# Weight sums released block by block, output stores on ScalarE's queue, and two buffers for the second group's blocks

## The chip, the cores and the metric

The kernel runs on one core of a Trainium2 chip. A core has TensorE (PE, matrix products), VectorE (DVE), ScalarE (ACT), GpSimd (POOL) and SyncE (SP), which here issues every transfer between the chip's main memory (DRAM) and the on-chip memory (SBUF). Products accumulate in PSUM banks. Each engine works through its own list of instructions in order; semaphores tie the lists together. The metric is the time of one execution in device microseconds, the median of several runs.

## The reference

One layer of an encoder works on two sequences, a prompt of 1024 tokens and a sample of 256, with a model width of 2048, all in float32:

```python
hn = rmsnorm(x, norm_w)
proj = jnp.einsum('btd,dp->btp', hn, w_in)          # 9232 columns
att = neighbourhood_attention(na_q, na_k, na_v, na_rpb)   # 8 heads of 128
att = (att * jax.nn.silu(na_g)).astype(x.dtype)
qk = jax.nn.silu(centred_depthwise_conv(ml_qk, conv_w, conv_b))
h = bidirectional_mlstm(mq, mk, mv, gates)          # 4 heads of 256
h = rmsnorm(h, head_norm_w)
mem = (h * jax.nn.sigmoid(ml_o) * jax.nn.silu(ml_z)).astype(x.dtype)
mixed = jnp.concatenate([att, mem], axis=-1)
y = x + jnp.einsum('btm,md->btd', mixed, w_out)     # then a final rmsnorm
```

The attention lets a token on a grid 64 wide see a window of 8 rows and 16 columns, with a learned bias. The mLSTM is a gated linear recurrence, done forwards and backwards in chunks.

## The kernel before

Each float32 operand is split into a high and a low half (`split`, lines 151 to 157: ScalarE copies the high half on line 153, VectorE takes the difference on line 154), and a product is three matmuls of halves. The 1280 tokens are worked on in a first part of 768 and a second of 512. Large products use a seven-product scheme for 2x2 blocks (Strassen-Winograd), which needs sums and differences of blocks of both operands.

The stages, in the order of the program:

1. The first part's projections (`first_tiles`, `pair_a`), until about 1120 us. Results go to DRAM tensors `pT`, `vD`, `cD`.
2. A loop over `ML_H` = 4 (line 1160). Turn i projects the second part's columns for two attention heads and one mLSTM head (`proj_v`, `proj_pair`, matmuls on lines 497 and 579; weights through two buffers tagged `wraw`), and then `run` (line 1134) weaves two streams together: the mLSTM units of head i and the attention of heads 2i and 2i+1. An attention head is one sample unit, `setup`, and four prompt blocks (`block`, line 707). A block scores, takes the softmax, transposes, multiplies by the values into a PSUM bank `b`, and writes its gated result (lines 750 and 753); the fourth stores the head to `mixT` (line 755).
3. After each `run`, eight calls of `wsum_unit` (line 1146). A unit loads 512 KB of the output weights `w_os` into the only buffer of tag `wsum`, forms four sums and differences on GpSimd in place (lines 1151 to 1154), and stores them to `sD` (line 1156). All 32 units prepare the block sums of the output weights.
4. `late_gate`: gate projections of the second part, multiplied into `mixT` (lines 548 and on). Between them `build` prepares the sums of the activations for the first output group of 512 tokens, through one buffer `bld` (line 1192), into tiles of the pool `comb`, which takes the place of the attention pool `att`.
5. The output projection (line 1265): group 0 for both column pairs (`G00`, `G01`), then the 256 sample tokens (`S`, whose activations `xs` are loaded on line 1374 through the buffers `po`), then group 1 (`G10`, `G11`), whose blocks are built in pieces during and after `S`. `w_tiles` loads and splits weights; `put` adds the products to `y` and the residual `xr`; `done` squares on ScalarE into a `po` buffer `jk`; `finish` (line 1293) scales a row of tiles by the norm and stores it on line 1305.

The order of the instructions on each engine is not written by hand. A scheduler fixes it at build time by simulating the program: an instruction is placed when its inputs and its buffer are free in the simulation and its engine is idle. Everything inside `run` has raised priority; the weight sums have not, and depend on nothing but their buffer. Tiles with one tag share that tag's buffers, and a new tile waits until all work on the old one in its buffer is over. On the chip each engine follows the fixed order, whatever comes late.

The lines that the change touches are the units and the place that calls them, the blocks of attention, the two masks (lines 462 to 465), `build`, `finish`, and the number of `po` buffers, `NPO`, on line 29.

Of the kernel before, what the change touches and what calls it, by code (L numbers as in the profile page):

```python
# [8 lines left out]
F32 = mybir.dt.float32  # L9
F32R = mybir.dt.float32r  # L10
AF = mybir.ActivationFunctionType
ALU = mybir.AluOpType

P = 128
# [11 lines left out]
HALF = GA // 2  # L26
NU = 8
VW = 258
NRA, NWS, NWT, NPC, NPO = 3, 8, 4, 5, 5
NAK = 384  # L30
KC0 = (0, 8, 24, 32)
BKIND = (0, 1, 1, 2)
# [6 lines left out]
def kernel(  # L39
# [24 lines left out]
    def f(ap):  # L64
        return ap.bitcast(F32)
# [390 lines left out]
    for _ in bg:  # L456
# [2 lines left out]
    wb, xp0 = pools  # L459

    late = ctx.enter_context(tc.tile_pool(name="late", bufs=1))
    mask_f, mask_b = (
        tri(late.tile([P, P], F32, tag=n, name=n), cm, 0, (0.0, NEG))
        for n, cm in (("mask_f", -1), ("mask_b", 1))
    )

    xp1 = ctx.enter_context(tc.tile_pool(name="xp1", bufs=1))

# [129 lines left out]
    att_ctx = ExitStack()  # L598
    ap = att_ctx.enter_context(tc.tile_pool(name="att", bufs=2))

    def hf(name):
        return ap.tile([P, 1032], F32R, tag="hf", name=name, bufs=8)

# [25 lines left out]
    def na_transpose(nm, st, order, dst):  # L629
        b = bank("a", f"{nm}t")  # L630
        n = len(order)
        for i, c in enumerate(order):
            PE.transpose(b[:, i * P : (i + 1) * P], st[:, c * P : (c + 1) * P], ident)
        bv = b[:, : n * P].rearrange("p (k q) -> p k q", q=P)
        S.copy(dst[0], bv)
        V.tensor_tensor(dst[1], bv, f(dst[0]), op=ALU.subtract)

    def na_sample(h):
        nm = f"nas{h}"
# [43 lines left out]
    def na_prompt(h):  # L683
        nm = f"nap{h}"
        hd = {}

        def setup():
            t = na_tile("nqk", [P, 4, TP], f"{nm}qk", 1, F32R)
            q, k = ([t[:, 2 * i + z] for z in range(2)] for i in range(2))
            for half in range(2):  # L690
                cs = slice(half * 512, half * 512 + 512)
                for w_, t, src in (("q", q, pT[QT0 + h]), ("k", k, pT[KT0 + h])):
                    raw = na_tile("nraw", [P, 512], f"{nm}{w_}r{half}", 2)
                    DM.dma_start(raw, src[:, cs])
                    if w_ == "q":
                        d = [
                            x_[:, cs].rearrange("p (b r c) -> p r b c", b=4, c=16) for x_ in t
                        ]
                        split(*d, raw.rearrange("p (r b c) -> p r b c", b=4, c=16))
                    else:  # L700
                        split(t[0][:, cs], t[1][:, cs], raw)
            o = na_tile("not", [P, TP], f"{nm}o", 1)
            DM.dma_start(o[:, :GA], pT[GT0 + h][:, :GA])
            hd["q"], hd["k"], hd["o"] = q, k, o
            yield

        def block(c4):
            q, k = hd["q"], hd["k"]
            n2 = f"{nm}_{c4}"
            kc = KC0[c4]  # L710
            kv = [x_.rearrange("p (r c) -> p r c", c=64) for x_ in k]
            st = [
                na_softmax(
                    f"{n2}_{rh}",
                    lambda a_: q[a_][:, rh * 512 + c4 * P : rh * 512 + (c4 + 1) * P],
                    lambda b_: kv[b_][:, 4 * rh : 4 * rh + 12, kc : kc + 32],
                    NAK, h, (BKIND[c4] * 2 + rh) * NAK,
                )
                for rh in range(2)
            ]  # L720
            v = na_tile("nv", [P, 2, 512], f"{n2}v", 2, F32R)
            raw = na_tile("nraw", [P, 512], f"{n2}vr", 2)
            vs = vD[h // 2][:TP, (h % 2) * P : (h % 2 + 1) * P].rearrange("(r c) d -> r c d", c=64)
            for m in range(4):
                DM.dma_start(raw[:, m * P : (m + 1) * P], vs[4 * m : 4 * m + 4, kc : kc + 32, :])
            split(v[:, 0], v[:, 1], raw)
            yield
            pt = na_tile("npt", [P, 2, 768], f"{n2}pt", 1, F32R)
            for rh in range(2):
                na_transpose(  # L730
                    f"{n2}_{rh}", st[rh], ((1, 2, 0), (0, 1, 2))[rh],
                    [
                        pt[:, z].rearrange("p (s r q) -> p s r q", r=2, q=P)[:, :, rh, :]
                        for z in range(2)
                    ],
                )
            yield
            b = bank("a", f"{n2}o")
            parts = ((1, 0, 256, 0), (2, 256, 256, 0), (0, 512, P, 0), (3, 640, P, P))
            for j, (m, src, n, o) in enumerate(parts):  # L740
                for i, (a_, b_) in enumerate(((0, 0), (0, 1), (1, 0))):
                    PE.matmul(
                        b[:, o : o + n], v[:, a_, m * P : (m + 1) * P], pt[:, b_, src : src + n],
                        start=j == 0 and i == 0, stop=j == 3 and i == 2,
                    )
            ov = hd["o"].rearrange("p (r c) -> p r c", c=64)
            bv = b[:, :256].rearrange("p (r c) -> p r c", c=16)
            cs = slice(c4 * 16, c4 * 16 + 16)
            ng = GA // 64
            V.scalar_tensor_tensor(  # L750
                ov[:, :ng, cs], bv[:, :ng], 0.5, ov[:, :ng, cs], op0=ALU.mult, op1=ALU.mult
            )
            S.copy(ov[:, ng:, cs], bv[:, ng:])
            if c4 == 3:
                DM.dma_start(mixT[h][:, :TP], hd["o"])
            yield

        yield setup()
        for c4 in range(4):
            yield block(c4)  # L760
# [382 lines left out]
                        if next(u_, "end") == "end":  # L1143
                            act.remove(u_)

    def wsum_unit(u):
        cp, kk, half = u // 16, u // 2 % 8, u % 2
        t = ap.tile([P, 4, 256], F32, tag="wsum", name=f"wsum{u}", bufs=1)
        DM.dma_start(t.rearrange("p s c -> p (s c)"), w_os[u])
        a11, a12, a21, a22 = (t[:, i] for i in range(4))  # L1150
        G.tensor_tensor(a22, a21, a22, op=ALU.add)  # L1151
        G.tensor_tensor(a21, a11, a21, op=ALU.subtract)
        G.tensor_tensor(a11, a22, a11, op=ALU.subtract)
        G.tensor_tensor(a12, a12, a11, op=ALU.subtract)  # L1154
        c0 = kk * 512 + half * 256
        DM.dma_start(sD[cp][:, :, c0 : c0 + 256], t)

    X = LazyX()
    rbs[1] = late.tile([P, GB], F32, tag="rstdb1", name="rstdb1")
    for i in range(ML_H):  # L1160
        proj_v(4 + i, X)
        if i == 0:
            x_stats(1, lambda c: mid(f"xdg1_{c}", 256))
        for n in (QK0 + 8 + 2 * i, QK0 + 2 * i):
            proj_pair(n, X)
        if i == 0:
            with tc.high_priority():
                tris = ml_tris()
                gates = {sq: ml_gates(sq, tris) for sq in ("p", "s")}
        proj_v(i, X)  # L1170
        for n in (QT0 + 2 * i, KT0 + 2 * i):
            proj_pair(n, X)
        run(
            [u for sq in ("s", "p") for u in ml_units(sq, i, gates[sq])],
            [u for h in (2 * i, 2 * i + 1) for u in (na_sample(h), *na_prompt(h))],
        )
        for u in range(8 * i, 8 * i + 8):
            wsum_unit(u)
    att_ctx.close()
    comb = ctx.enter_context(tc.tile_pool(name="comb", bufs=1))  # L1180
    SG = 256
# [7 lines left out]

    def build(g, C, kk, parts):  # L1190
        nm = f"bd{g}{parts[0]}{kk}"
        bl = comb.tile([P, 1024], F32, tag="bld", name=nm)
        s0, s1 = bl[:, :512], bl[:, 512:]
        for z, s_ in enumerate((s0, s1)):
            DM.dma_start(s_, mixT[kk + 8 * z][:, g * 512 : g * 512 + 512])
        for kind in parts:
            C[kind, kk] = comb_tile(kind, kk, f"cm{g}")
        b11, b12, d1, t3 = s0[:, :SG], s0[:, SG:], s1[:, :SG], s1[:, SG:]

        def put(kind, src):  # L1200
            t = C[kind, kk]
            if kind != "b":
                t = t.rearrange("p h c t -> p h (c t)")
            split(t[:, 0], t[:, 1], src)

        if "b" in parts:
            put("b", b11)
        if "u" in parts:
            put("u", s1)
        if "w" in parts:  # L1210
            V.tensor_tensor(s1, s1, s0, op=ALU.subtract)
        else:
            V.tensor_tensor(t3, t3, b12, op=ALU.subtract)
        if "v" in parts:
            V.tensor_tensor(b12, b12, b11, op=ALU.subtract)
            V.tensor_tensor(b11, t3, b11, op=ALU.add)
            put("v", s0)
        if "w" in parts:
            V.tensor_tensor(d1, d1, t3, op=ALU.subtract)
            put("w", s1)  # L1220
# [72 lines left out]
    def finish(t):  # L1293
# [5 lines left out]
        for i in range(D // w_):  # L1299
# [2 lines left out]
                S.mul(yt[:, cs], yt[:, cs], rs)  # L1302
            else:
                V.tensor_scalar(yt[:, cs], yt[:, cs], rs, None, op0=ALU.mult)
            DM.dma_start(y[t * P : (t + 1) * P, cs], yt[:, cs])

    def add(o, a_, b_):
        V.tensor_tensor(o, a_, b_, op=ALU.add)
# [179 lines left out]
```

## Time and profile before

| what | value |
|---|---|
| median of 3 runs | 2721.89 us (2718.3 to 2723.4) |
| the profiled execution | 2715.22 us, span 2713.5 us |
| instructions | 43634 |
| mean granted TensorE clock | 0.987 |
| TensorE busy | 96% of the span |
| VectorE, ScalarE, GpSimd busy | 72%, 51%, 27% |
| moved by DMA | 454.21 MB, mean 167 GB/s |

The span is cut into rows of instructions, each with a start and a length. A line of the views below names the engine, the source line, the operation and the tiles it writes and reads. Where an engine sat idle, the view of waits names the instruction that ended the idle time; "idle before" is that time. `SPq` is the queue on which SP issues transfers; a transfer's own landing appears as `DMA`. The granted clock is a share of TensorE's full speed.

### The profile page before, as it was taken

What the parts mean: (1) busy time and instruction counts of PE and PEld (TensorE: products, weight loads), DVE (VectorE), ACT (ScalarE), POOL (GpSimd) and SP (SyncE); (2) the same over time, 40 slices, a digit from 0 to 9 for tenths busy, and PEclk for the clock granted to TensorE, in tenths of its full rate; (3) what the DMA queues carried; (4) which work ended last, traced back from release to release, by engine and by line L of the source; (5) the groups of instructions that cost most, each with busy time, mean ns of one, the idle gap of its engine ahead of it and who ended that gap; (6) DMA issues with size and microseconds to landing.
All of it is one profiled execution on the core that took longest, in us unless ns stands there. A gap on an engine that the chain in (4) does not pass through costs nothing.

```text
span 2713.5 us, 43634 instructions
## 1 busy us (share of the span) xinstructions
PE 2611.9 (96%) x14518; PEld 2386.9 (88%) x14518; DVE 1963.3 (72%) x3902; ACT 1385.1 (51%) x3132; POOL 731.5 (27%) x1025
## 2 busy tenths in 40 slices
PE   8999999999999999988989999999999999989997
PEld 8999999999999999977878989889888887867776
DVE  7867878788787878863677587677676675777786
ACT  7534444444444444522645565665565443555554
POOL 0434444444444444233233210000010000120112
PEclk9999999999999999999989999999999999999999
DMA  6423333322323232656767755655655456778875
GB/s 208 149 74 123 110 126 106 98 94 94 106 94 106 90 105 93 205 187 205 246 209 232 246 176 178 204 168 170 197 159 160 148 187 230 217 232 264 285 234 181
DMA packets 258042, 454.21 MB, mean 167 GB/s; under 512 B 30320, under 2 KB 138008, under 8 KB 257816
## 3 DMA queue, kind: packets, MB, share of 16 engines
q1 hardware_dynamic: 257816, 451.42, 51.5%
q8 instruction: 114, 1.87, 0.3%
q14 instruction: 112, 0.92, 0.1%
HBM read 368.41 MB, written 82.91 MB: 166 GB/s over the span
## 4 chain that ended last, share of the span: by engine, by line
PE 35%; DMA 14%; DVE 5%; ACT 3%; POOL 2%; issue 2%; SPq 1%; POOLq 0%; ACTq 0%; DVEq 0%
PE pc L497 14%; PE G01p L1265 3%; PE G11p L1265 3%; PE G00p L1265 3%; PE pv L579 2%; DMA wsum<-in_w_os_dram 2%; DMA sD<-wsum 2%; PE G10p L1265 1%; PE S L1265 1%; DMA wr<-in_w_in_dram 1%; PE A52b L190 1%; DMA pT<-pco 1%; DMA nap_0vr<-vD 1%; POOL wsum L1154 1%; DMA bd1b<-mx 1%
## 5 line engine op out<-in xcount | busy, mean ns | idle before, releaser
L154 DVE TENSOR_TENSOR ws<-wr,ws 128x512 fp32r<-128x512 f32 x224 | 161.1, 722 | 96.0 <-ACT ws L153 94.5
L153 ACT CAST ws<-wr 128x512 fp32r<-128x512 f32 x224 | 138.0, 619 | 139.4 <-PE pc L497 81.6
L1288 POOL TENSOR_TENSOR y<-y,fn 128x512 f32<-128x512 f32 x40 | 61.7, 1554 | 522.0 <-ACT jk L1287 491.0
L1151 POOL TENSOR_TENSOR wsum<-wsum 128x256 f32<-128x256 f32 x32 | 26.5, 828 | 240.7 <-DMA wsum<-in_w_os_dram 204.3
L154 DVE TENSOR_TENSOR wsv<-wr_v,wsv 128x512 fp32r<-128x512 f32 x64 | 46.1, 726 | 30.8 <-ACT wsv L153 30.5
L1265 PE MATMUL S<-ws_S,xsb 128*128 128x512 f32 x192 | 48.9, 410 | 13.1 <-ACT xsb L153 10.7
L154 DVE TENSOR_TENSOR ws_G01w<-wrG01w,ws_G01w 128x512 fp32r<-128x512 f32 x56 | 44.5, 807 | 20.0 <-ACT ws_G01w L153 18.6
L1265 PEld LDWEIGHTS S<-ws_S,xsb 128*128 128x128 f32 x192 | 37.0, 196 | 24.5 <-ACT xsb L153 11.1
L153 ACT CAST wsv<-wr_v 128x512 fp32r<-128x512 f32 x64 | 38.8, 614 | 38.2 <-DMA wr_v<-in_w_in_dram 24.0
L154 DVE TENSOR_TENSOR ws_G11w<-wrG11w,ws_G11w 128x512 fp32r<-128x512 f32 x56 | 44.9, 820 | 16.5 <-ACT ws_G11w L153 16.1
L153 ACT CAST ws_G11w<-wrG11w 128x512 fp32r<-128x512 f32 x56 | 34.6, 619 | 36.6 <-PE G11p L1265 29.8
L153 ACT CAST ws_G01w<-wrG01w 128x512 fp32r<-128x512 f32 x56 | 34.7, 620 | 35.3 <-PE G01p L1265 28.5
L154 DVE TENSOR_TENSOR ws_S<-wrS,ws_S 128x512 fp32r<-128x512 f32 x64 | 46.2, 739 | 7.6 <-ACT ws_S L153 7.2
L276 DVE SCALAR_TENSOR_TENSOR pcv<-pco,cw_sb,pcv 128x516 f32<-128x516 f32 x64 | 49.0, 774 | 3.4 <-ACT pcv L270 3.3
L154 DVE TENSOR_TENSOR ws_G00w<-wrG00w,ws_G00w 128x512 fp32r<-128x512 f32 x48 | 37.1, 789 | 15.1 <-ACT ws_G00w L153 13.7
L1265 PE MATMUL S<-ws_S,xsv 128*128 128x512 f32 x192 | 46.2, 396 | 1.2 <-ACT ws_S L153 1.0
L497 PE MATMUL pc<-x_10h,ws 128*128 128x512 f32 x112 | 45.6, 407 | 0.0
L1265 PEld LDWEIGHTS S<-ws_S,xsv 128*128 128x128 f32 x192 | 35.7, 188 | 11.1 <-ACT ws_S L153 1.9
L154 DVE TENSOR_TENSOR ws_G10w<-wrG10w,ws_G10w 128x512 fp32r<-128x512 f32 x56 | 40.0, 742 | 7.1 <-ACT ws_G10w L153 7.0
L497 PE MATMUL pc<-x_11h,ws 128*128 128x512 f32 x112 | 45.2, 403 | 0.0
L153 ACT CAST ws_G00w<-wrG00w 128x512 fp32r<-128x512 f32 x48 | 29.6, 620 | 30.2 <-PE G00p L1265 27.6
L497 PE MATMUL pc<-x_0h,ws 128*128 128x512 f32 x112 | 45.0, 401 | 0.0
(1737 smaller groups left out, 9168.9 us busy)
## 6 DMA issues: line engine op xcount, KB each, us to landing
wr<-in_w_in_dram SPq DMA_DIRECT2D x112, 512.0 KB
wr_v<-in_w_in_dram SPq DMA_DIRECT2D x32, 512.0 KB
wsum<-in_w_os_dram SPq DMA_DIRECT2D x32, 512.0 KB
sD<-wsum SPq DMA_DIRECT2D x32, 512.0 KB
wrS<-in_w_o_dram SPq DMA_DIRECT2D x64, 256.0 KB
xq<-in_xtok_dram SPq DMA_DIRECT2D x20, 512.0 KB
xr<-in_xtok_dram SPq DMA_DIRECT2D x40, 256.0 KB
wrG00w<-sD SPq DMA_DIRECT2D x32, 256.0 KB
```

The lines of the kernel that those rows point to most:

```text
L153: S.copy(hi, src)
L154: V.tensor_tensor(lo, src, f(hi), op=ALU.subtract)
L190: PE.matmul(o, w(a_), x(b_), start=first and m == 0, stop=last and m == 2)
L276: V.scalar_tensor_tensor(dst[:, a:n], src[:, a + j - pad : n + j - pad], cw_sb[:, ct, j : j + 1], dst[:, a:n], op0=ALU.mult, op1=ALU.add,)
L497: PE.matmul(pb[j], t[:, wi, c : c + P], xs, start=r == 0 and f_ == 0 and q == 0 and wi == 0 and xs is xh, stop=r == 3 and f_ == 1 and q == ...
L579: PE.matmul(outs[tt], xs[:, tt * P : (tt + 1) * P], t[:, wi, q * w : (q + 1) * w], start=first and m == 0 and (gates or tt % 2 == 0), stop ...
L1151: G.tensor_tensor(a22, a21, a22, op=ALU.add)
L1154: G.tensor_tensor(a12, a12, a11, op=ALU.subtract)
L1265: PE.matmul(bk[s_], x_[:, xi, s_ * P : (s_ + 1) * P], t[:, wi, :512], start=first and m == 0, stop=last and m == 2,)
L1288: G.tensor_tensor(yc, yc, fn[nb], op=ALU.mult)
```

## The change

- `wsum_unit` moves ahead of the attention code and takes a second argument, `pace`. Before its load it copies one column of `pace` into its buffer on ScalarE. Each attention block calls one unit, number 4h + c4 for block c4 of head h, with its own PSUM bank as `pace`, right after its last copy. The eight calls after each `run` are gone. The sums run inside `run`, at its priority.
- `finish` first scales all pieces of a row and then stores them, last piece first, and the stores are issued by ScalarE.
- `build` for the second group takes one of the two `wraw` buffers for odd blocks and `bld` for even ones.
- `NPO` goes from 5 to 6. The masks `mask_f` and `mask_b` move from the pool `late` to the pool `att`.

```diff
-NRA, NWS, NWT, NPC, NPO = 3, 8, 4, 5, 5
+NRA, NWS, NWT, NPC, NPO = 3, 8, 4, 5, 6
...
     late = ctx.enter_context(tc.tile_pool(name="late", bufs=1))
-    mask_f, mask_b = (
-        tri(late.tile([P, P], F32, tag=n, name=n), cm, 0, (0.0, NEG))
-        for n, cm in (("mask_f", -1), ("mask_b", 1))
-    )
...
     ap = att_ctx.enter_context(tc.tile_pool(name="att", bufs=2))
 
+    mask_f, mask_b = (
+        tri(ap.tile([P, P], F32, tag=n, name=n, bufs=1), cm, 0, (0.0, NEG))
+        for n, cm in (("mask_f", -1), ("mask_b", 1))
+    )
...
+    def wsum_unit(u, pace):
+        cp, kk, half = u // 16, u // 2 % 8, u % 2
+        t = ap.tile([P, 4, 256], F32, tag="wsum", name=f"wsum{u}", bufs=1)
+        S.copy(t[:, 0, 0:1], pace)
+        DM.dma_start(t.rearrange("p s c -> p (s c)"), w_os[u])
+        a11, a12, a21, a22 = (t[:, i] for i in range(4))
+        G.tensor_tensor(a22, a21, a22, op=ALU.add)
+        G.tensor_tensor(a21, a11, a21, op=ALU.subtract)
+        G.tensor_tensor(a11, a22, a11, op=ALU.subtract)
+        G.tensor_tensor(a12, a12, a11, op=ALU.subtract)
+        c0 = kk * 512 + half * 256
+        DM.dma_start(sD[cp][:, :, c0 : c0 + 256], t)
...
             S.copy(ov[:, ng:, cs], bv[:, ng:])
+            wsum_unit(4 * h + c4, b[:, 0:1])
             if c4 == 3:
                 DM.dma_start(mixT[h][:, :TP], hd["o"])
...
-        for u in range(8 * i, 8 * i + 8):
-            wsum_unit(u)
     att_ctx.close()
...
-        bl = comb.tile([P, 1024], F32, tag="bld", name=nm)
+        if g and kk % 2:
+            bl = wb.tile([P, 1024], F32, tag="wraw", name=nm, bufs=2)
+        else:
+            bl = comb.tile([P, 1024], F32, tag="bld", name=nm)
...
                 V.tensor_scalar(yt[:, cs], yt[:, cs], rs, None, op0=ALU.mult)
-            DM.dma_start(y[t * P : (t + 1) * P, cs], yt[:, cs])
+        for i in reversed(range(D // w_)):
+            cs = slice(i * w_, i * w_ + w_)
+            S.dma_start(y[t * P : (t + 1) * P, cs], yt[:, cs])
```

The old `wsum_unit(u)`, without the copy and the argument, is removed from its place behind `run`.

11 lines of the change are left out of this document (removed).

## The prediction

> **What bounds the kernel now.** I read the page first, then the busy time by stretch, then who waits for whom on TensorE and on SP's queue, then the timelines round the longest waits. The page says who is nearest to full:
>
> ```profile
> span 2713.5 us, 43634 instructions
> PE 2611.9 (96%) x14518; PEld 2386.9 (88%) x14518; DVE 1963.3 (72%) x3902; ACT 1385.1 (51%) x3132; POOL 731.5 (27%) x1025
> ```
>
> TensorE is idle for 2713.5 - 2611.9 = 101.6 us, and only that can be won without removing matmuls; the change removes none. The same table by stretch (columns: stretch; busy us of PE, weight load, DVE, ACT, POOL; granted clock; share of the DMA engines; GB/s) shows where it lies:
>
> ```profile
> 1120.00:1300.00 180.00, 160.29 (x912) 140.03 (x911) 97.92 (x230) 61.84 (x121) 57.62 (x97) 0.94 0.62 204
> 1300.00:1600.00 300.00, 278.94 (x1748) 252.25 (x1747) 207.71 (x484) 176.71 (x436) 86.54 (x164) 0.96 0.70 226
> 1600.00:2140.00 540.00, 533.06 (x3251) 474.05 (x3250) 379.29 (x977) 331.27 (x811) 44.06 (x143) 1.00 0.55 172
> 2420.00:2540.00 120.00, 105.67 (x436) 82.20 (x436) 87.15 (x148) 67.01 (x131) 18.68 (x18) 0.96 0.80 265
> 2540.00:2714.00 174.00, 154.77 (x657) 121.92 (x655) 127.26 (x196) 88.98 (x164) 33.18 (x30) 0.97 0.70 233
> ```
>
> Idle is 19.7 us in 1120 to 1300 and 21.1 in 1300 to 1600, but 6.9 in the 540 us after that (0.013 per us), although the same attention and projection work runs there. Then 14.3 and 19.2 us in the output stage. The 32 weight sums run exactly in the two poor stretches. Their row, and the chain of waits, which in that stretch is a string of load, sum, store (first and thirteenth load of the string):
>
> ```profile
> L1149 SPq DMA_DIRECT2D wsum<-in_w_os_dram x32: 327/333/438, 1126.2 to 1558.6; - x32
> 1126.17 4.83 DMA wsum<-in_w_os_dram
> 1270.65 3.63 DMA wsum<-in_w_os_dram
> ```
>
> Twelve units between these two make (1270.65 - 1126.17) / 12 = 12.0 us a unit: with one buffer the units follow each other, each issued by SP in order. TensorE's waits there, and SP's own waits at the units' two DMAs:
>
> ```profile
> PE nas_0s L616 <- ACT nas0qk L153: 8.1, 1, 8.1
> PE mgsa L839 <- DVE mgstmp L833: 4.8, 1, 4.8
> PE mls_0s L920 <- ACT mls_0q L156: 3.7, 1, 3.7
> PE mgsi L812 <- DVE mgpri L840: 3.2, 1, 3.2
> PE mlp_1in L920 <- ACT mlp_1Cf L153: 4.0, 1, 4.0
> SPq L1156 <- POOL wsum L1154: 54.5, 17, 5.0
> SPq L1149 <- DMA sD<-wsum: 47.0, 24, 4.1
> SPq L1156 <- DMA wsum<-in_w_os_dram: 31.2, 16, 5.0
> ```
>
> SP stands 54.5 + 47.0 + 31.2 = 133 us in front of a weight sum's load or store. How that reaches TensorE is seen at its longest wait, 8.1 us:
>
> ```profile
> 1277.27 0.68 DVE L167 TENSOR_TENSOR pco<-pc,rstdb 128x512 f32<-128x512 f32 x1
> 1277.97 0.53 SPq L1156 DMA_DIRECT2D sD<-wsum  x1
> 1281.17 0.34 SPq L1149 DMA_DIRECT2D wsum<-in_w_os_dram  x1
> 1282.04 0.90 SPq L524 DMA_DIRECT2D pT<-pco  x2
> 1287.82 0.32 SPq L643 DMA_DIRECT2D nas0r<-pT  x1
> 1280.00:1300.00 20.00, 11.95 (x77) 11.74 (x76) 6.74 (x20) 6.67 (x16) 4.03 (x9) 0.74 0.75 242
> ```
>
> The projection is ready at 1277.95; its store is issued 4.1 us later, since SP first waits for the sum's store to land; the read-back waits for that store, and the matmuls for the read-back. The granted clock is 0.74 in this window, so the gap costs more than its length.
>
> **The change, part by part.**
>
> *A, weight sums leave 1120 to 1300.* Each is now started by an attention block, the first at about 1345. Of the 19.7 us of idle the gate chain keeps 4.8 + 3.2 = 8.0 (VectorE's own), and 180 x 0.013 = 2.3 stays as elsewhere: 9.4 can go. The clock loses 0.06 x 180 = 10.8 us; half of it I put into idle time, and of the other half the same share 9.4 / 19.7: 2.6. A = 12.0 faster; bounds 3 (only the 4.1 us less what the store's landing still costs) and 20.
>
> *B and C, the same units beside attention.* The block ends, as ScalarE's copies show:
>
> ```profile
> L753 ACT COPY nap1o<-nap_0o x1: 213/213/213, 1492.1 to 1492.1; 128x64 f32<-128x64 f32 x1
> L753 ACT COPY nap3o<-nap_0o x1: 220/220/220, 1701.4 to 1701.4; 128x64 f32<-128x64 f32 x1
> L753 ACT COPY nap3o<-nap_3o x1: 212/212/212, 1722.0 to 1722.0; 128x64 f32<-128x64 f32 x1
> L753 ACT COPY nap7o<-nap_3o x1: 212/212/212, 2139.1 to 2139.1; 128x64 f32<-128x64 f32 x1
> ```
>
> By the order of heads and blocks 10 units fall before 1600 where 18 of them start now, and 22 after it where none do. Idle of 1300 to 1600 above the later rate is 21.1 - 3.9 = 17.2 us, plus half of the clock's 0.04 x 300 = 12 us at the share 17.2 / 21.1: 4.9. That is 22.1 / 18 = 1.23 us a unit. B: 8 units fewer, 9.8 faster. C: 22 units put into a stretch that has next to no idle. They come one per (2139 - 1602) / 22 = 24 us against one per 15, and a unit hurts when SP is still late from the last one, so I scale the price by the density twice, 0.63 x 0.63 = 0.4: 22 x 1.23 x 0.4 = 10.8 slower; bounds 0 and 27 (full price). The four POOL sums, some 3.3 us a unit, go into a POOL that is busy 44 of 540 us; behind a sum waiting for its load stand the row scales (L104, L105) and mask sums (L997) of the mLSTM units, as now.
>
> *D, the added wait.* The pace copy (one column, about 0.2 us by the 128x64 copies above, 32 of them 6.4 us on an engine busy 331 of 540) writes the only buffer, so it waits on ScalarE until the previous unit's store has landed. Behind it stand splits and exponentials, for which VectorE and then TensorE wait, and the block's PSUM bank stays held. Blocks of a head's second half follow each other every (1722.0 - 1701.4) / 3 = 6.9 us, less than the unit's 12.0. The order is fixed at build time with such a wait foreseen, so what hurts is the error: SP's waits on the same landing are 47.0 / 24 = 2.0 us each. Half the blocks follow that closely: 16 x 2.0 = 32 us of ScalarE; its cover is the splits it has ready ahead of TensorE, so I take a tenth, 3 slower; bounds 0 and 60 (four such heads, each 3 x 12.0 - 20.6 = 15.4 us late, all of it reaching TensorE). With 12 us units the last sum ends near 2139 + 24 = 2163, when the attention pool can close. That delays the blocks of the first output group:
>
> ```profile
> L1195 SPq DMA_DIRECT2D bd0b<-mx x16: 319/398/432, 2144.5 to 2217.5; - x16
> 2138.43 128.18 PE pc L497 x553
> ```
>
> They are issued until 2217.5, and TensorE has gate projections until 2266.6: a delay of 24 us is hidden behind some 40. Without that cover it would cost 24.
>
> *E, output stage.* TensorE's longest wait of all is here, with the SP order before it and the first load's landing:
>
> ```profile
> PE S L1265 <- ACT xsb L153: 10.7, 1, 10.7
> 2425.07 2.94 SPq L1305 DMA_DIRECT2D out_dram<-y  x4
> 2432.71 3.04 SPq L1374 DMA_DIRECT2D xs<-mx  x5
> 2432.71 5.55 DMA xs<-mx
> L1305 SPq DMA_DIRECT2D out_dram<-y x24: 332/460/1182, 2425.1 to 2708.9; - x24
> ```
>
> Four output stores of 512 KB go out on SP ahead of the sample group's tiles. On ScalarE's queue they take 2.9 us of issue out of SP's way, and their 2 MB no longer stand ahead of the loads in one queue; five loads come at once because the shared buffers are five, and there will be six. Against it, 24 x 0.46 = 11.0 us of issue go to ScalarE, two to four of them just when it must split these tiles. I take 4 faster for this wait, bounds 0 and 10.7. The trace has no store on ScalarE's queue; an issue is bounded by 0.33 and 1.18 us, and I take SP's median. Elsewhere the 11 us lie beside an engine busy 67 of 120 and 89 of 174 us; if a tenth shows, 1 slower. The Trainium skill, DMA: Bandwidth & Descriptors, section Issuing engines are not separate DMA queues, says that queues of different engines share the same 16 DMA engines and that a second issuer saves issue time only; by it this wait would shrink by the 2.9 us of issue alone. No run before the change shows the other queue.
>
> The second group's blocks load through two buffers instead of one. TensorE's waits after 2540 on operands of the second group are small:
>
> ```profile
> PE G10p L1265 <- DVE ws_G10w L154: 2.5, 3, 1.3
> PE G10p L1265 <- ACT cm1b L153: 0.9, 1, 0.9
> ```
>
> So 2 faster at best 3.4; below nothing too, to -3, since two blocks in flight load DMA engines that are 0.80 busy. The tail: the last products end before 2700, and then come
>
> ```profile
> 2704.50 2.56 ACT L1302 ACTIVATE y<-y,rs 128x512 f32<-128x512 f32 x4 [3.28 <-POOL rs L105]
> 2696.29 13.19 SPq L1305 DMA_DIRECT2D out_dram<-y  x12
> ```
>
> SP finishes issuing at 2709.5. ScalarE needs 2.56 + 8 x 0.46 = 6.2 us from 2704.5: 2710.7, 1 slower. SP's waits for y there hold up nothing, for nothing is behind them. E = 4 - 1 + 2 - 1 = 4 faster. The two masks move to another pool with the same four POOL instructions: nothing.
>
> Sum: 12.0 + 9.8 - 10.8 - 3 + 4 = 12.0 faster. The profiled execution took 2715.2 us (span 2713.5), 6.7 under the median of 2721.9; off the median, 2710.
>
> **The rivals.**
>
> *The relief is paid back in full.* A unit costs 1.23 us wherever it runs, because SP is in order in both. Then C is 27: 12.0 + 9.8 - 27 - 3 + 4 = -4, 2726, or with E's upper bound about 2719. For it: SP's loads are as needed in 1600 to 2140. Against it: that stretch has one unit per 24 us.
>
> *Nothing is paid back.* C and D are 0 and E reaches 10: 2721.9 - 32 = 2690. For it: ScalarE runs ahead of TensorE in 1600 to 2140, and DMA is at 0.55. Against it: the copy's wait is new.
>
> *ScalarE's queue becomes the bound.* The copy's place in ScalarE's order is the mechanism: a late store holds every split behind it. Half of D's 60 us with the rest as forecast gives 2710 - 3 + 30 = 2737. It decides once more than a quarter of the 60 us reaches TensorE (15 against the 12 + 3 won). For it: four tight heads, PSUM banks held meanwhile. Against it: waits foreseen in the order; ScalarE is busy 61%.
>
> *The queue move does nothing*, as the skill's rule has it: the forecast less some 2 us, 2712; same sign.
>
> **How the numbers follow.** Forecast, with the queue rule's case, 0.42 (2700 to 2718); nothing paid back 0.18; paid back in full 0.15; ScalarE bound 0.25. A difference under 0.2% (5.4 us) can't be told from none. Faster: 0.18 and most of the forecast's 0.42, 0.55 in all. Same: the forecast's upper edge and most of the paid-back case, 0.15. Slower: the rest, 0.30. Range: from 2680 (a little below the nothing-paid case) to 2742 (a little above the ScalarE case).
>
> **What would show it.** Right: no weight sum before 1340, SP's waits at the two DMAs under 133 us, the 8.1 us wait of nas_0s at most half, idle of 1120 to 1600 near 20 us, idle after that up by about 10. Wrong: ScalarE waiting at the pace copy for stores with TensorE idle right behind, the first group's blocks running past the last gate projection, or stores on ScalarE's queue ahead of late splits before the sample group.

## The result and the profile after

| | before | after |
|---|---|---|
| median of 20 runs | 2718.68 us (2713.18 to 2723.4) | 2722.48 us (2718.96 to 2727.22) |
| ratio after / before | | 1.0016, 95% interval 1.0009 to 1.0023 |

The changed kernel is about 4 us slower, within the 0.2% that the prediction called no change; the forecast was 12 us faster. The two profiled executions differ by 11 us (2715.2 and 2726.3, one 3.5 us under its kernel's median and the other 3.8 over), so some of the differences below are theirs and not the change's.

The first two lines of the page of the changed kernel:

```profile
span 2724.6 us, 43685 instructions
PE 2617.1 (96%) x14518; PEld 2393.5 (88%) x14518; DVE 1965.2 (72%) x3902; ACT 1388.5 (51%) x3164; POOL 734.2 (27%) x1025
```

TensorE is idle for 107.5 us, against 101.6. The busy time by stretch of the changed kernel (columns as in the prediction), and then one row of the kernel before that the prediction did not need:

```profile
1120.00:1300.00 180.00, 179.22 (x1115) 159.18 (x1114) 105.88 (x274) 82.03 (x171) 12.00 (x55) 1.00 0.48 150
1300.00:1600.00 300.00, 280.20 (x1719) 252.69 (x1718) 205.25 (x495) 174.16 (x441) 64.33 (x134) 0.96 0.63 197
1600.00:2140.00 540.00, 515.29 (x3021) 454.75 (x3021) 362.99 (x897) 308.03 (x762) 103.57 (x200) 0.97 0.63 198
2140.00:2420.00 280.00, 269.03 (x1176) 217.55 (x1175) 183.94 (x302) 124.14 (x236) 28.68 (x26) 0.98 0.66 211
```

```profile
2140.00:2420.00 280.00, 278.02 (x1194) 225.12 (x1193) 189.32 (x295) 127.52 (x229) 20.39 (x13) 0.99 0.63 205
```

Idle of TensorE went from 19.7 to 0.8 us in 1120 to 1300, stayed (21.1 to 19.8) in 1300 to 1600, and rose from 6.9 to 24.7 in 1600 to 2140 and from 2.0 to 11.0 in 2140 to 2420. The granted clock moved with it: 0.94 to 1.00 in the first row, 1.00 to 0.97 in the third. The poor stretch did not go; it moved to where the sums went. Three tile rows of the changed kernel date it: the loads of the sums, the end of the last attention block, and the loads of the first output group's blocks (columns: duration of one in ns, minimum, median and maximum; then the starts of the first and the last in us):

```profile
L643 SPq DMA_DIRECT2D wsum<-in_w_os_dram x32: 327/334/400, 1315.9 to 2178.6; - x32
...
L767 ACT COPY nap7o<-nap_3o x1: 212/212/212, 2169.3 to 2169.3; 128x64 f32<-128x64 f32 x1
...
L1199 SPq DMA_DIRECT2D bd0b<-mx x16: 319/374/433, 2189.4 to 2268.8; - x16
```

The first sum waits for the first attention block, as meant. The kernel's first block ends 30 us earlier than before (1315.3 against 1345.5), and its last one 30 us later (2169.3 against 2139.1). Much of that is a new order only: by 2140 both kernels have kept TensorE busy equally long (972.3 and 974.7 us over the three stretches). The start of `G00`, behind all of it, tells the loss: 2278.7 against 2268.7.

Some of TensorE's longest waits in the changed kernel, and then SP's and ScalarE's at the sums (us in total, times, longest):

```profile
PE S L1269 <- ACT xsb L153: 14.2, 1, 14.2
...
PE mlp_1in L935 <- ACT mlp_1Cf L153: 8.0, 4, 3.6
PE mlp_1in L935 <- ACT mlp_1Cb L153: 7.4, 2, 5.1
...
PE mlp_0acc L935 <- ACT wsum L642: 5.2, 2, 4.3
PE nas_0s L617 <- ACT nas2qk L153: 4.8, 1, 4.8
...
PE nas_1s L617 <- ACT wsum L642: 3.2, 1, 3.2
...
SPq L650 <- POOL wsum L648: 48.6, 16, 5.7
...
SPq L643 <- DMA sD<-wsum: 24.8, 12, 2.7
...
SPq L650 <- DMA wsum<-in_w_os_dram: 21.9, 12, 3.1
...
ACT wsum L642 <- DMA sD<-wsum: 44.4, 9, 7.6
```

SP still stands 95.3 us at the sums by these rows (133 before), and another 9.0 us at their loads for the pace copy: part of the wait at the load has become ScalarE's 44.4 us at that copy. What stands behind SP is seen in the timeline just after the first blocks (start, length, in us; the rows of SP and of GpSimd):

```profile
1353.11 0.43 SPq L473 DMA_DIRECT2D wr_v<-in_w_in_dram  x1
...
1354.98 0.72 POOL L647 TENSOR_TENSOR wsum<-wsum 128x256 f32<-128x256 f32 x1
1357.39 1.32 POOL L1012 TENSOR_TENSOR mlp_2dm<-mlp_2al,mask_f 128x128 f32<-128x128 f32 x2 [1.69 <-DVE mlp_1p L154]
...
1359.55 0.73 POOL L648 TENSOR_TENSOR wsum<-wsum 128x256 f32<-128x256 f32 x1
...
1360.31 0.53 SPq L650 DMA_DIRECT2D sD<-wsum  x1
1360.88 0.63 SPq L473 DMA_DIRECT2D wr_v<-in_w_in_dram  x1
1361.60 1.42 SPq L919 DMA_DIRECT2D mlp_3kcv<-cD  x2
```

From 1353.5 to 1360.3 SP issues nothing: its next instruction is the sum's store, and GpSimd has mask sums, themselves late, between the third and the fourth step of the sum. Weights of the next projection and operands of the next mLSTM unit leave only after it. It is the wait on SP that stood behind the prediction's 8.1 us, found again beside the attention. How far this one delay reaches is not shown: ScalarE then waits 4.9 us for one of those operands, `mlp_3kcv`, but TensorE is busy for all of 1360 to 1370.

### The profile page after: what moved, and what is told of

Same layout as the page of the kernel before. It is cut to its first block, busy times and chain, and to the rows that moved or that the text cites. A ratio compares the mean times of both kernels' runs of the same rounds, so it can differ in the third digit from the quotient of the medians.

```text
span 2724.6 us, 43685 instructions
## 1 busy us (share of the span) xinstructions
PE 2617.1 (96%) x14518; PEld 2393.5 (88%) x14518; DVE 1965.2 (72%) x3902; ACT 1388.5 (51%) x3164; POOL 734.2 (27%) x1025
## 4 chain that ended last, share of the span: by engine, by line
PE 37%; DMA 10%; DVE 6%; issue 3%; ACT 2%; POOL 2%; SPq 1%; ACTq 0%; POOLq 0%; DVEq 0%
PE pc L493 11%; PE pv L575 4%; PE S L1269 3%; PE G00p L1269 3%; PE G11p L1269 3%; PE G01p L1269 2%; PE G10p L1269 2%; DMA wr<-in_w_in_dram 1%; PE A54b L190 1%; DMA wsum<-in_w_os_dram 1%; PE A52b L190 1%; DMA sD<-wsum 1%; DMA lt<-mx 1%; DVE ws L154 1%; DMA bd0b<-mx 1%
## 5 line engine op out<-in xcount | busy, mean ns | idle before, releaser
L1269 PE MATMUL S<-ws_S,xsb 128*128 128x512 f32 x192 | 47.5, 407 | 14.2 <-ACT xsb L153 14.2
L154 DVE TENSOR_TENSOR ws_G01w<-wrG01w,ws_G01w 128x512 fp32r<-128x512 f32 x56 | 44.5, 806 | 19.9 <-ACT ws_G01w L153 18.5
L154 DVE TENSOR_TENSOR ws_G11w<-wrG11w,ws_G11w 128x512 fp32r<-128x512 f32 x56 | 44.9, 820 | 16.9 <-ACT ws_G11w L153 16.7
L153 ACT CAST ws_S<-wrS 128x512 fp32r<-128x512 f32 x64 | 39.2, 619 | 32.6 <-PE S L1269 27.9
L153 ACT CAST wsv<-wr_v 128x512 fp32r<-128x512 f32 x64 | 39.2, 616 | 28.5 <-PE pc L493 13.2
L154 DVE TENSOR_TENSOR ws_G10w<-wrG10w,ws_G10w 128x512 fp32r<-128x512 f32 x56 | 43.3, 791 | 14.2 <-ACT ws_G10w L153 13.8
L493 PE MATMUL pc<-x_6h,ws 128*128 128x512 f32 x112 | 45.4, 405 | 5.7 <-ACT ws L153 5.7
L153 ACT CAST ws_G10w<-wrG10w 128x512 fp32r<-128x512 f32 x56 | 34.2, 618 | 29.0 <-PE G10p L1269 20.8
L493 PE MATMUL pc<-x_4h,ws 128*128 128x512 f32 x112 | 45.8, 409 | 2.6 <-DVE ws L154 1.5
L493 PE MATMUL pc<-x_7h,ws 128*128 128x512 f32 x112 | 45.2, 404 | 0.0
```

The source lines that it names most:

```text
L153: S.copy(hi, src)
L154: V.tensor_tensor(lo, src, f(hi), op=ALU.subtract)
L493: PE.matmul(pb[j], t[:, wi, c : c + P], xs, start=r == 0 and f_ == 0 and q == 0 and wi == 0 and xs is xh, stop=r == 3 and f_ == 1 and q == ...
L1269: PE.matmul(bk[s_], x_[:, xi, s_ * P : (s_ + 1) * P], t[:, wi, :512], start=first and m == 0, stop=last and m == 2,)
```

## The experiments

Ratios are against the kernel before, with 95% intervals; a difference in us is that ratio less one, times 2718.

**The parts alone.** The theory on record has the moved sums 8 us faster and the rest 4 us faster; the rivals put the loss on ScalarE's pace copy, on the new queue, or on a full payback.

Only the moved sums, with the pace copy (stores, builds, masks and `NPO` as before):

```diff
+            wsum_unit(4 * h + c4, b[:, 0:1])
...
-        for u in range(8 * i, 8 * i + 8):
-            wsum_unit(u)
```

> The kernel before with only the weight sums moved into the attention blocks (paced by ScalarE's copy). Theory 1, the sums cost what they cost in the changed kernel wherever the rest stands: TensorE reaches the end of the first output group 16 us later, as it does there (2366.5 against 2350.0), so 14 to 18 us slower. Theory 2, the loss is made by the other parts (a larger number of shared buffers changes the built order): about 10 us faster, as I had predicted for the sums alone (12.0 + 9.8 - 10.8 - 3 = 8).

1.0014 (1.0005 to 1.0023), 4 us slower: neither of the two theories' ranges, but a loss as large as that of the whole change from the moved sums alone. The stretches:

```profile
1120.00:1300.00 180.00, 179.03 (x1121) 159.45 (x1121) 105.44 (x274) 81.65 (x167) 10.52 (x55) 1.00 0.49 152
...
1600.00:2140.00 540.00, 515.85 (x3051) 454.73 (x3051) 368.35 (x916) 314.24 (x781) 106.58 (x204) 0.98 0.64 200
```

18.7 us more of TensorE's time in the first, 17.2 us less in the last. `G00` starts at 2269.5, where it started before (2268.7): by these two traces, what the sums cost ahead of the output stage they cost in the new place too.

Only the stores on ScalarE's queue:

```diff
-            DM.dma_start(y[t * P : (t + 1) * P, cs], yt[:, cs])
+        for i in reversed(range(D // w_)):
+            cs = slice(i * w_, i * w_ + w_)
+            S.dma_start(y[t * P : (t + 1) * P, cs], yt[:, cs])
```

> The kernel before with only the output stores moved to ScalarE's queue. If the stores on ScalarE's queue make the longer wait before the sample group (14.2 us instead of 10.7), 3 to 4 us slower and that wait near 14. If they give the shorter sample stage (90.7 us instead of 97.3), 4 to 6 faster. My prediction had 4 - 1 - 1 = 2 faster for this part.

0.9994 (0.9984 to 1.0004): no difference that can be told. TensorE's wait ahead of `S` is 13.2 us here against 10.7, so the longer wait comes with the stores; it isn't seen in the time.

Only the two buffers for the second group's blocks:

```diff
-        bl = comb.tile([P, 1024], F32, tag="bld", name=nm)
+        if g and kk % 2:
+            bl = wb.tile([P, 1024], F32, tag="wraw", name=nm, bufs=2)
+        else:
+            bl = comb.tile([P, 1024], F32, tag="bld", name=nm)
```

> The kernel before with only the second buffer for the second group's blocks. Predicted 2 faster. If this part is what shortens the sample stage and the second group (97.3 to 90.7 and 83.3 to 80.5 us), 5 to 9 faster; if two blocks in flight make the wait before the sample group longer, that wait is near 14 us and the gain is less.

0.9979 (0.9969 to 0.9989), 6 us faster.

Only the sixth `po` buffer, with the masks in `att`:

```diff
-NRA, NWS, NWT, NPC, NPO = 3, 8, 4, 5, 5
+NRA, NWS, NWT, NPC, NPO = 3, 8, 4, 5, 6
...
-        tri(late.tile([P, P], F32, tag=n, name=n), cm, 0, (0.0, NEG))
+        tri(ap.tile([P, P], F32, tag=n, name=n, bufs=1), cm, 0, (0.0, NEG))
```

> The kernel before with only the sixth shared buffer and the masks in the attention pool. Expected 0 to 3 faster: six sample tiles load at once instead of five, so the 10.7 us wait shrinks by at most one landing; if the sixth buffer reorders the projections, a difference of either sign appears before 2140 us, where the other single parts show none.

0.9987 (0.9976 to 0.9997), 3.5 us faster. The four parts alone add up to 4 - 2 - 6 - 3.5 = 7 us faster, and together they are 4 slower: some of them must hurt each other. Two further kernels split them. The moved sums with the sixth buffer (the edits of the first and the last diff above):

> The kernel before with the sums moved and the sixth shared buffer (and the masks). The single parts gave +4 and -3.4 us. If parts add up: 1 us slower than before. If these two disturb each other (the changed kernel is 11 us slower than the sum of its single parts, and its first output group starts 9 us later than with the units alone): about 10 us slower, with that group starting near 2279 us instead of 2269.

1.0055 (1.0041 to 1.0069), 15 us slower, where the two alone give +4 and -3.5. Its long stretch:

```profile
1600.00:2140.00 540.00, 511.04 (x3002) 450.85 (x3001) 359.05 (x895) 307.00 (x761) 106.77 (x200) 0.98 0.63 197
```

Idle is 29.0 us there, and its last block ends at 2169.6, 15 us after that of the moved sums alone (2154.5). And everything but the moved sums (the last three diffs together):

> The changed kernel with the sums left where they were before: stores on ScalarE's queue, two buffers, the sixth shared buffer. By the single parts (-1.4, -6.2, -3.4): 11 us faster than before, the sample stage and the second group as short as in the changed kernel (90.7 and 80.5 us). If these parts win the same microseconds twice: 6 faster.

0.9959 (0.9947 to 0.9972), 11 us faster, just the sum of its parts. So the change is 11 us won by the rest and, on top of the rest, 15 us lost by the moved sums, which alone lose 4.

**What a sum costs, and with what.** All 32 sums left out (no load, no sum, no store; the products read plain blocks of the weights in place of summed ones):

```diff
-        for u in range(8 * i, 8 * i + 8):
-            wsum_unit(u)
...
-                src = sD[cp][:, WSUM[i]]
+                src = w_o[2 * cp + WSUM[i] // 2][:, WSUM[i] % 2 * 4096 : WSUM[i] % 2 * 4096 + 4096]
```

> The kernel before without the 32 weight sums: they are left out, and the four summed products read plain blocks of the output weights instead, so the same bytes are loaded in the output stage. Gives the price of all sums where they stood: by my price of 1.23 us for 18 units and 12 us for the first 14, 34 us faster; by the relief seen in the changed kernel between 1120 and 1300 us (18.9 us of busy time and the clock's 10.8), 35 to 45 faster. If the idle time of 1120 to 1600 has other causes, under 15.

0.9805 (0.9792 to 0.9818), 53 us faster, more than any of the expected ranges. That is 53 / 32 = 1.65 us a sum, for work that lies on GpSimd and the DMA engines and never on TensorE. Nearly all of it lies ahead of the output stage, as `G00` starts 49.5 us sooner (2219.2 against 2268.7). Its stretches:

```profile
1120.00:1300.00 180.00, 178.81 (x1119) 159.20 (x1118) 105.27 (x273) 81.46 (x167) 10.53 (x55) 1.00 0.49 152
1300.00:1600.00 300.00, 292.69 (x1876) 264.52 (x1875) 218.93 (x540) 189.08 (x465) 30.23 (x94) 0.99 0.56 173
```

In the first row the gate chain's 8.0 us, which the prediction took for VectorE's own, are gone as well. The timeline of the kernel before shows what stood behind the larger of its two waits, 4.8 us at `mgsa` (in brackets the idle time before, and what ended it):

```profile
1192.84 0.58 SPq L1156 DMA_DIRECT2D sD<-wsum  x1
...
1194.14 0.94 SPq L904 DMA_DIRECT2D mls_0kcv<-cD  x1
...
1198.47 0.63 ACT L156 ACTIVATE mls_0k<-mls_0kcv 128x512 fp32r<-128x512 f32 x1 [4.45 <-DMA mls_0kcv<-cD]
...
1199.13 0.69 DVE L157 SCALAR_TENSOR_TENSOR mls_0k<-mls_0kcv,mls_0k 128x512 fp32r<-128x512 f32 x1 [4.30 <-ACT mls_0k L156]
...
1200.54 0.17 DVE L833 TENSOR_TENSOR mgstmp<-mgstmp 128x16 f32<-128x16 f32 x1
```

SP issues nothing from 1189.0 to 1192.8, where it stands at a sum's store. Only then does it issue the load `mls_0kcv`; ScalarE and VectorE wait for that load's split, and the step that `mgsa` needs (L833) comes behind the split in VectorE's list.

Is the price in the bytes? The kernel before, with 16 of each 256 columns loaded, summed and stored, and the products reading plain blocks:

```diff
-        DM.dma_start(t.rearrange("p s c -> p (s c)"), w_os[u])
-        a11, a12, a21, a22 = (t[:, i] for i in range(4))
+        DM.dma_start(t[:, :, 0:16], w_os[u].rearrange("p (s c) -> p s c", s=4)[:, :, 0:16])
+        a11, a12, a21, a22 = (t[:, i, 0:16] for i in range(4))
...
-        DM.dma_start(sD[cp][:, :, c0 : c0 + 256], t)
+        DM.dma_start(sD[cp][:, :, c0 : c0 + 16], t[:, :, 0:16])
```

> The kernel before with the same 32 units, waits and queues, but each moves and sums only 16 of its 256 columns per block; the other columns are left out and the summed products read plain blocks of the output weights. If the 33.5 MB make the price: within 10 us of the kernel without sums, 43 to 53 faster. If SP's waits make it: the waits shrink from about 4 to about 2 us a time, so 20 to 30 faster.

0.9965 (0.9952 to 0.9978), 9 us faster, under both expected ranges. A sixteenth of the bytes saves 9 of the 53 us. The tile row of the loads and the first stretch say why:

```profile
L1149 SPq DMA_DIRECT2D wsum<-in_w_os_dram x32: 539/567/611, 1126.2 to 1361.5; - x32
```

```profile
1120.00:1300.00 180.00, 152.55 (x840) 131.30 (x839) 82.33 (x210) 55.09 (x107) 41.74 (x140) 0.92 0.45 118
```

The sums still follow each other, now (1361.5 - 1126.2) / 31 = 7.6 us apart, and TensorE is idle for 27.5 us of 180 with the DMA engines 0.45 busy. What hurts, then, is mostly a chain of load, sum and store that the in-order queues of SP and GpSimd pass through, and not its bytes. The test is not a pure one, since the small transfers go in pieces of 64 bytes where the full ones have rows of 4 KB.

**Does the added wait of ScalarE carry the loss?** The changed kernel with the pace copy on GpSimd, reading the block's gated result:

```diff
-        S.copy(t[:, 0, 0:1], pace)
+        G.tensor_copy(t[:, 0, 0:1], pace)
...
-            wsum_unit(4 * h + c4, b[:, 0:1])
+            wsum_unit(4 * h + c4, hd["o"][:, ng * 64 + c4 * 16 : ng * 64 + c4 * 16 + 1])
```

> The changed kernel with the pace copy on GpSimd, read from the head's result tile instead of the PSUM bank: ScalarE waits for no store and no bank is held. If ScalarE's wait (44.4 us in 9 waits) and the held banks make the loss, 12 to 18 us faster than the changed kernel and its TensorE idle of 1600 to 2140 back near 10 us. If every unit has its price through SP's order, within 4 us of the changed kernel.

0.9991 (0.998 to 1.0002), some 7 us faster than the changed kernel, between the two expected ranges. So ScalarE's wait, with the held bank, costs about 7 us, near the 5.2 + 3.2 = 8.4 that TensorE's two rows on `wsum L642` show directly. But the long stretch is not cured:

```profile
1600.00:2140.00 540.00, 515.52 (x3072) 455.61 (x3071) 368.21 (x915) 311.79 (x760) 113.61 (x221) 0.98 0.63 198
```

24.5 us idle, as with the copy on ScalarE. Next suspect: the last sums, which keep the attention pool open after the last block. The kernel just shown, with each head's sums started one step earlier, by its sample unit and its first three blocks:

```diff
+        wsum_unit(4 * h, o[:, 0:1])
...
-            wsum_unit(4 * h + c4, hd["o"][:, ng * 64 + c4 * 16 : ng * 64 + c4 * 16 + 1])
+            if c4 < 3:
+                wsum_unit(4 * h + 1 + c4, hd["o"][:, ng * 64 + c4 * 16 : ng * 64 + c4 * 16 + 1])
```

> The changed kernel with the pace copy on GpSimd, and the units given to each head's sample unit and first three blocks, so that the last unit starts one block sooner and only three follow each other. If the late closing of the attention pool (24 us after its last block) still costs time at the first output group: that group's first load comes about 12 us sooner after the last block and the kernel is 4 to 8 us faster than with the pace on GpSimd alone, so 7 to 11 faster than before. If the loss is in the stretch 1600 to 2140 itself: no change against it (2 to 3 faster than before).

0.9998 (0.9989 to 1.0008). The first block of the output stage is loaded 14.8 us after the last attention block instead of 23.5, and no time is gained: the late closing of the pool is not the cost by itself.

**SP's queue.** The sum's store waits on SP for GpSimd. Issued by GpSimd, which has just finished the sum, it waits for nothing. First in the kernel before, sums in their old place:

```diff
-        DM.dma_start(sD[cp][:, :, c0 : c0 + 256], t)
+        G.dma_start(sD[cp][:, :, c0 : c0 + 256], t)
```

> The kernel before with the store of each sum issued by GpSimd right behind its last sum, where it needs no wait; loads stay on SP. SP loses its waits at the stores (86 of 133 us), GpSimd gets no new one. If SP's in-order waits are the price of the sums: 15 to 30 us faster. If the price is the sums' share of the DMA engines or of the memory ports: within 5 us of before.

0.9973 (0.9962 to 0.9984), 7 us faster, between the two expected ranges. The wait moved on, to SP at the next load:

```profile
SPq L1149 <- DMA sD<-wsum: 129.0, 26, 10.8
```

SP's wait at the sums is nearly as long as before (129 against 133 us), so the total of SP's waits isn't the price by itself.

The same single edit in the changed kernel, where the blocks release the sums:

> The changed kernel with one edit: each sum's store is issued by GpSimd behind its last sum instead of by SP. If SP's waits at these stores are the price of the moved units: 15 to 25 us faster than the changed kernel, so 11 to 21 faster than before. If ScalarE's pace copy or the place of the units matters as much: under 8 faster than the changed kernel.

0.9927 (0.9914 to 0.9941), 20 us faster than before and about 24 faster than the changed kernel. One line turns the loss into a gain (this profiled execution, 2705.25 us, is 9 us over its kernel's median, so its rows show less than the gain):

```profile
1300.00:1600.00 300.00, 288.54 (x1830) 261.49 (x1830) 217.10 (x513) 181.76 (x456) 81.65 (x150) 0.98 0.66 209
1600.00:2140.00 540.00, 515.73 (x3024) 454.58 (x3023) 361.91 (x908) 310.85 (x779) 122.04 (x222) 0.98 0.63 198
```

The idle time of 1300 to 1600 falls from 19.8 to 11.5 us. That of 1600 to 2140 stays at 24.3, but that row covers less of what was slow: the last block ends at 2139.7 instead of 2169.3. SP still waits at the loads (`ACT` is the pace copy):

```profile
SPq L643 <- DMA sD<-wsum: 74.4, 16, 8.8
ACT wsum L642 <- DMA sD<-wsum: 45.2, 10, 7.8
```

Load and store both issued by GpSimd, in the kernel before, so that SP has no part in the sums:

```diff
-        DM.dma_start(t.rearrange("p s c -> p (s c)"), w_os[u])
+        G.dma_start(t.rearrange("p s c -> p (s c)"), w_os[u])
...
-        DM.dma_start(sD[cp][:, :, c0 : c0 + 256], t)
+        G.dma_start(sD[cp][:, :, c0 : c0 + 256], t)
```

> The kernel before with both transfers of each weight sum issued by GpSimd, which also does the sums, so that SP never waits for them; bytes and places stay. If SP's in-order waits (133 us) are how the sums reach TensorE, 20 to 30 us faster and idle of 1120 to 1600 near 15 us instead of 41. If it is the load on the DMA engines, within 5 us of before.

1.0023 (1.0012 to 1.0034), 6 us slower, outside both expected ranges. GpSimd now stands where SP stood, and packed sums keep it there:

```profile
POOL wsum L1151 <- DMA wsum<-in_w_os_dram: 128.8, 32, 6.4
POOL wsum L1149 <- DMA sD<-wsum: 109.4, 30, 6.2
```

The same queue with the sums released block by block: first the kernel with the pace on GpSimd and the sums one step earlier, with the store alone issued by GpSimd.

> The same with each sum's store issued by GpSimd, so that SP waits for no sum. If SP's waits at the sums' stores are what units cost beside attention: 5 to 15 us faster than the run without it, and TensorE's idle of 1600 to 2140 (24.5 us with the pace on GpSimd) under 15. If they are not: within 4 us of it.

0.9899 (0.9886 to 0.9912), 27 us faster than before and faster than without that edit (0.9998) by the same, more than expected. Idle of 1300 to 1600 is 10.5 us (16.9 without it). In 1600 to 2140 it is 19.5, where under 15 was expected; SP's 69.3 us at the loads stand there still. Then the load too:

> The fastest version so far (pace and store on GpSimd, units at the sample unit and three blocks) with the load issued by GpSimd too, so that SP has no part in the sums. SP still waits 69.3 us at the loads there. If every wait of SP at a sum has its price: 5 to 10 us faster than that version. If the waits on GpSimd for the loads' buffer hurt as when both transfers stood on its queue before (6 slower than before): 5 to 30 slower than that version.

0.9855 (0.9837 to 0.9872), median 2674.34 us, 39 us faster than before: the fastest kernel here that still forms the sums. It is some 10 to 14 us (by the medians and by the ratios) above the one without any sums, but that one lacks the other three parts of the change, worth 11 us. By the start of `G00`, ahead of which the sums cost their time, it is 16.5 us behind (2235.7 against 2219.2).

```profile
1300.00:1600.00 300.00, 291.17 (x1871) 263.77 (x1870) 220.55 (x531) 186.31 (x456) 86.05 (x180) 0.99 0.69 216
1600.00:2140.00 540.00, 529.59 (x3086) 465.35 (x3086) 372.45 (x913) 312.45 (x763) 140.36 (x268) 0.99 0.64 204
```

```profile
POOL wsum L645 <- DMA wsum<-in_w_os_dram: 126.2, 27, 6.2
POOL wsum L642 <- DMA sD<-wsum: 48.1, 12, 5.8
```

GpSimd waits 174 us at the sums instead of SP, TensorE's idle time is 8.8 and 10.4 us in the two rows, and the DMA engines move more per second than in the changed kernel. Against the kernel at 0.9998 these are the same 32 sums with the same bytes, released by the same blocks: the edit names only another engine to issue their transfers, and 39 us hang on it. The order fixed at build time changes with such an edit, though: the lists of matmuls of these two kernels agree up to the 7744th of 14518 and then part. How much of a single difference is the wait and how much the new order is not separated. That the issuer matters rests on four pairs that differ by the store's issuer alone, each faster with GpSimd: by 7 (before), 24 (changed), 27 (sums one step earlier) and 7 us (the next kernel).

The store's queue with the three good parts, sums in their old place (everything but the moved sums, store issued by GpSimd):

> The sums where they were before, their stores issued by GpSimd, and the other parts of the change (stores of the output on ScalarE's queue, two buffers, sixth shared buffer). If the parts add up: -11.1 - 6.9 = 18 us faster than before (ratio 0.993). If the store on GpSimd and the sixth buffer disturb each other as the moved sums and the sixth buffer did: 5 to 10 faster.

0.9932 (0.9919 to 0.9945), 18.5 us faster: 11 + 7, additive. It is also as fast as the changed kernel with the same store edit (0.9927): with the store on GpSimd's queue, the move of the sums by itself costs nothing and wins nothing.

## Why the prediction was wrong

*A, the stretch that the sums leave: right, too small.* 12.0 was forecast. TensorE's busy time there rose by 18.9 us and the clock went to 1.00. The step that kept 8.0 us for the gate chain as VectorE's own was wrong: both rows are gone in the changed kernel, in the one with the moved sums alone and in the one without sums, and the larger one stood behind a load that SP issued late.

*B, 1300 to 1600: wrong.* 9.8 us were to come from 8 sums fewer at a price of 1.23. Twelve started there instead of 17 (the tile rows by stretch count 17, not the 18 of the forecast), and the idle time above the later rate went from 17.2 only to 15.9 us. That is 1.3 us a sum after, 1.0 before, so the price of one sum was not a constant either.

*C, the sums beside attention: the step that failed.* "I scale the price by the density twice" made 10.8 of a full 27. The idle time of 1600 to 2140 rose by 17.8 us, for the 16 sums that start in it: 1.1 us each, unscaled, before the clock's loss of 0.03 of 540 us is counted. The 24 us between sums, from which the scaling came, is an average over bunches and the pauses between them. The sums come in fours, one four to a head; the loads of one such four in the changed kernel:

```profile
L643 SPq DMA_DIRECT2D wsum<-in_w_os_dram x4: 332/334/337, 1675.7 to 1712.8; - x4
```

That is (1712.8 - 1675.7) / 3 = 12.4 us from one to the next, as close as the 12.0 of the kernel before; the mean of each of the eight fours lies between 10.9 and 18.9 us, against 15 in 1300 to 1600 before. The prediction itself has blocks 6.9 us apart under D and did not use it here. So the waits were not spread thinner where they fall, and whether sums that really stand apart would cost less isn't shown. Nor need a sum follow closely on another to hurt: in the timeline SP stands 6.8 us at a store because GpSimd has other work between. The rival "paid back in full" gives the right total with the right reason, SP in order in both places; that its 2726 lies so near is partly luck, since its A was 7 us too small (18.9 of busy time against 12.0) and its B 8 too large (1.3 less idle time against 9.8). The single edit that takes the store from SP gives 24 us back in the changed kernel.

*D, the added wait: right in kind, too small.* 3 us were forecast, 7 measured with the copy elsewhere. That the pool's late closing would be covered held for the closing alone. The first blocks' loads came 45 us later (2189.4 against 2144.5), not 24, since the attention itself ended 30 us later; then `G00` starts 10 us late, and the row of 2140 to 2420, in which it lies, shows 9 us more idle time.

*E, the output stage: right sign, wrong rows.* Instead of 4, the three parts alone won 11. The wait ahead of `S`, from which the 4 were to come, did not shrink: 13.2 us with the stores alone and 10.9 with the sixth buffer alone, against 10.7. In the whole change, by the first and last matmul of each stage, the sample stage is 6.6 us shorter and `G10` 2.8, and the gap ahead of `S` is longer: the wait for `xs` grew from 10.7 to 14.2. Its six loads do leave one behind the other, but ScalarE is not free for the first split until 2458.9 (timeline of the changed kernel; in brackets the idle time before, and what ended it):

```profile
2449.62 3.91 SPq L1380 DMA_DIRECT2D xs<-mx  x6
...
2454.30 1.15 ACT L1306 ACTIVATE y<-y,rs 128x1024 f32<-128x1024 f32 x1 [0.51 <-POOL rs L105]
...
2455.66 3.19 ACTq L1311 DMA_DIRECT2D out_dram<-y  x3
2458.90 1.94 ACT L153 CAST xsb<-xs 128x256 fp32r<-128x256 f32 x6 [2.40 <-issue]
```

ScalarE's splits stand behind a row's scaling and its store issues, the last of the things that the prediction named as able to make it wrong. The Trainium skill, DMA: Bandwidth & Descriptors, section Issuing engines are not separate DMA queues, says that a second issuing engine saves issue time only. The stores on ScalarE's queue agree with it: no difference that can be told (0.9994). The sums' store does not: there the issuing engine had a wait of its own to lose, and 7 to 27 us came with another issuer.

*The sum.* The parts were added as if they were independent. The moved sums and the sixth buffer are not: 15 us slower together, nothing by addition. What of the order fixed at build time makes this isn't settled. The trace shows the place (29.0 us idle in 1600 to 2140, a last block 15 us later) and not the cause. Also open is why 19.5 us of idle time stayed in 1600 to 2140 with the store alone on GpSimd's queue; with the load there too it was 10.4. Nor is it separated what GpSimd's own waits for the sums' loads cost (204 us before, 205 in the changed kernel, 126 in the fastest): mask sums and row scales of the mLSTM units stand behind them.

## What to carry to other kernels

Background transfers can cost more by where they stand than by their bytes: each waits in the in-order list of the engine that issues it, and holds what is queued behind it. So read from the timeline what stands behind such a wait, and look at the spacing of the transfers one by one, since an average rate hides that they come in bunches. Have a store issued by the engine that finished its data; that won in all four kernels here. A whole chain of load, work and store on that engine's queue won where the blocks released its units (39 us against SP's queue) and lost where each unit followed directly on the last (6 us). When background work is moved, price it in the new place at the full price of the old one until a run shows otherwise.

## What was not expected of the hardware

- The transfers that GpSimd issues hold that engine longer. In the fastest kernel a load takes 0.556 us of GpSimd and a store 0.736 (medians of 32), where SP spends 0.334 and 0.550 on the same ones in the changed kernel. It won nevertheless.

```profile
L643 POOL DMA_DIRECT2D wsum<-in_w_os_dram x32: 550/556/767, 1299.6 to 2112.8; - x32
...
L650 POOL DMA_DIRECT2D sD<-wsum x32: 722/736/752, 1310.3 to 2120.6; - x32
```

- The time of a sum falls much less than its bytes: 7.6 us from one to the next with a sixteenth of them (in pieces of 64 bytes), 12.0 with all.
- In 1120 to 1300 the granted clock was lower where TensorE idled more: 0.92 with 27.5 us idle of 180 in the kernel with few bytes, 0.94 with 19.7 in the kernel before, 1.00 with 0.8 in the changed one.
